# Layer 0 of a two-layer decoder trunk: the latents projected ahead of the last gated tiles and left unscaled, POOL's convolution taps moved to VectorE and 16 of them to TensorE

## The chip, the core and the metric

The kernel runs on one core of a Trainium2 chip. The time is the device time of one launch in microseconds. A core has five engines with a queue each, worked off in order: TensorE (PE, matrix products from SBUF into PSUM), VectorE (DVE), ScalarE (ACT), GpSimd (POOL, which does not touch PSUM here) and SyncE (SP, which issues the transfers). [...]

## What is computed

One sequence of 512 tokens with 1024 channels goes through two layers and a last RMSNorm. The change touches the mixer of layer 0 alone:

```python
def conv_mla_mixer(h, cos, sin, w_in, conv_w, conv_b, conv_ln_g, conv_ln_b,
                   q_norm_g, w_uq, kv_norm_g, w_ukv, w_out):
    proj = h @ w_in                                     # h = rmsnorm(x)
    a, g = proj[..., :512], proj[..., 512:1024]
    u = a * jax.nn.sigmoid(g)
    u = causal_dwconv(u, conv_w, conv_b)                # 31 taps, one filter per channel
    u = jax.nn.silu(layernorm(u, conv_ln_g, conv_ln_b)) # over the 512 channels
    cq, ckv, kr = ...                                   # 384, 256 and 32 columns of proj
    q = (rmsnorm(cq, q_norm_g) @ w_uq)                  # 8 heads of 64 + 32
    kv = (rmsnorm(ckv, kv_norm_g) @ w_ukv)              # 8 heads: 64 keys, 64 values
    ...                                                 # rotary on the 32 parts
    o = mla_attention(qn, qr, kn, kr, v)                # causal, blocks of 128 queries
    return jnp.concatenate([u, o], axis=-1) @ w_out
```

Behind the mixer follow a gated MLP with 2816 channels, a pooling mixer and a second MLP.

## The kernel before

Activations lie channel-major: a tile holds 128 channels by 512 tokens. A product that must be exact is made of three (`mm3`, lines 107 to 109): each operand is split into a rounded part `hi` (ScalarE, L96) and a rest `lo` (VectorE, L97). Weights stream through three buffers, one chunk ahead of the products (`weights`), and every chunk is split on its way. A few products take plain float32 operands in one instruction of the program, which the trace shows as two: scores (L503), values (L548), diagonals (L241) and the key fold (L559).

RMSNorm is applied late: the raw products lie in PSUM, and the factor of each token comes from sums of squares (`Squares`, `rstd`, `rsqrt`) on TensorE and then a chain of eleven tiny VectorE instructions (L192 to L199). `spread` turns a column of factors into rows: four diagonals on VectorE (L240), four products (L241), a copy (L245). `rows0` holds the factor of h.

The order in layer 0 is the order of the code, with the scheduler of the framework placing instructions on each engine by its own estimates:

1. `acc4`: the first two a tiles and the first two g tiles together; meanwhile `r0`, `rows0` and the rotary tables (`rotary`).
2. Four more projections, a and g of the tiles 2 and 3, each pair followed by `glu`.
3. Five projections of latents (`latent`: three of cq, two of ckv). Each is multiplied by `rows0` into a temporary t (L447), split (L101, L102), squared (L211) and summed (L213). The tenth projection is the rotary key.
4. `rstd` of both latents gives `r_q` and `r_kv`; then queries 0 and 1, the keys of the first pair (which need `r_kv` spread over rows), and four value tiles.
5. Eight heads: `scores` with a softmax (reduction with mask L506, its scaled negative L510, exponential L514, normalisation L522), `transposes` of the head before, `values` of the one before that, and the next queries and keys.
6. The output projection (`half`), with the LayerNorm of the convolution between (L614 to L639).

The convolution runs behind all this. `conv(m)` puts the taps of a tile into two lists, which `pump(nd, np_)` hands out at fixed places (`GLU`, `LAT`, `BLK`, `END` taps at a time). A VectorE tap (L367) adds to an accumulator in the PSUM bank `conv`, which ScalarE opens with the last tap and the bias (L361). A POOL tap is a product (L385) and a sum (L387) in SBUF. `close` (L390) adds the two. POOL has 12, 12, 12 and 16 taps of the four tiles, VectorE the other 68.

Of the kernel before, what the change touches and what calls it, by code (L numbers as in the profile page):

```python
# [38 lines left out]
WARM = 40  # L39
POOL_TAPS = (12, 12, 12, 16)  # L40
GLU, LAT, BLK, END = 2, 3, 1, 0


@with_exitstack
def kernel(
# [47 lines left out]

# [1 line left out]
    def split(dst, src):  # L95
# [21 lines left out]
    def rows_of(t, a, b):  # L117
        return t[a:b, 0, :], t[a:b, 1, :]

# [1 line left out]
    stream = (  # L121
        [(w_in0[k], 512) for k in range(KD)]
        + [(w_in1[m], 1024) for m in range(10)]
        + [(w_uq[0], 768), (w_ukv[0], 1024), (w_ukv[1], 1024)]
# [36 lines left out]

# [1 line left out]
    idle = p_c.tile([P, P], mybir.dt.bfloat16, name="idle")  # L163
# [7 lines left out]

# [1 line left out]
    col = p_c.tile([P, N_COL], F32, name="col")  # L173
# [8 lines left out]

# [1 line left out]
    held = []  # L184

    def behind(i):
        """Background work traced from here on starts after instruction i."""
        held[:] = [i]
# [14 lines left out]
    class Squares:  # L203
        """Sums of squares over the channels: tiles are added up, the last one apart."""

# [10 lines left out]

    def rstd(stats, blocks=range(4)):
        ps = aux()
        nb = len(blocks)
        v = small(nb * len(stats))  # L220
        for k, st in enumerate(stats):
            for i, b in enumerate(blocks):
                at = 2 * (nb * k + i)
                for n, t in enumerate(st.parts):
                    pe.matmul(  # L225
                        ps[:, at : at + 2], t[:, b * P : (b + 1) * P], ones[:, 0:2],
                        start=n == 0, stop=n == len(st.parts) - 1,
                    )
            dve.tensor_scalar(
                v[:, nb * k : nb * (k + 1)], ps[:, 2 * nb * k : 2 * nb * (k + 1) : 2],  # L230
                1.0 / st.n, EPS, op0=ALU.mult, op1=ALU.add,
            )
        return rsqrt(v, nb * len(stats))

    def spread_bank(r, blocks=2, tag="aux"):
        """Per-token column to rows: every partition gets the token's value."""
        ps = aux(tag)
        for i in range(blocks):
            d = p_t.tile([P, P], F32, tag="diag", bufs=4, name=uid("d"))
            dve.tensor_scalar(d, ident, r[:, i : i + 1], None, op0=ALU.mult)  # L240
            pe.matmul(ps[:, i * P : (i + 1) * P], ones, d, start=True, stop=True)  # L241
        return ps[:, : blocks * P]
# [6 lines left out]

    # ==== layer 0: conv + latent attention ====  # L250
    p_m = tc.alloc_tile_pool(name="mixer", bufs=1, side="left", reuse_waits="tile")
# [20 lines left out]

    # rotary tables: the turn of each angle from exact products with the digits of 1/(2 pi)
    pos_i = p_t.tile([P, 64], I32, tag="rope_i", bufs=1, name="pos_i")
# [53 lines left out]
    with tc.issue_after(opened.ins):  # L328
        for k in range(KD):
            stat.add(x[k])  # L330
    acc4 = [bank() for _ in range(4)]
    for k in range(KD):
        w = weights(2)
        for m in range(4):
            mm3(acc4[m], part(w, m), pair(xg[k]), k == 0, k == KD - 1)
        if k == 5:
            r0 = rstd([stat])
    rows0 = rows_tile()
# [9 lines left out]

    # depthwise conv, in the background: taps on DVE into PSUM, the rest on ACT and Pool
    u, ys = [], []  # L350
    dve_work, pool_work = [], []

    def conv(m):
# [11 lines left out]

        def dve_tap(j):
            i = dve.scalar_tensor_tensor(  # L367
                st["acc"], u[m][:, j : j + S], c(cw + j), st["acc"],
                op0=ALU.mult, op1=ALU.add,
            )  # L370
            if held:
                tc.add_manual_dep(
                    i.ins, held.pop().ins.name,
                    mybir.DependencyInfo(
                        mybir.DependencyClass.NoSync, mybir.DependencyReason.DATA
                    ),
                    reason="background",
                )

        def pool_tap(j):  # L380
            tap, w = u[m][:, j : j + S], c(cw + j).to_broadcast([P, S])
            t = side
            if j:
                t = p_m.tile([P, S], F32, tag="tapped", bufs=2, name=uid("tapped"))
            pool.tensor_tensor(t, tap, w, op=ALU.mult)  # L385
            if j:
                pool.tensor_tensor(side, side, t, op=ALU.add)  # L387

        def close():
            dve.tensor_tensor(side, st["acc"], side, op=ALU.add)  # L390

        pool_work.extend((lambda j=j: pool_tap(j)) for j in range(POOL_TAPS[m]))
        first = [True]

        def tap(j):
            if first[0]:
                open_acc()
                first[0] = False
            dve_tap(j)
            if j == CW - 2:  # L400
                close()

        dve_work.extend((lambda j=j: tap(j)) for j in range(POOL_TAPS[m], CW - 1))

    def pump(nd, np_):
        for _ in range(min(np_, len(pool_work))):
            pool_work.pop(0)()
        for _ in range(min(nd, len(dve_work))):
            dve_work.pop(0)()

    # GLU branch: u = a * sigmoid(g), kept behind CW - 1 zeros
    def glu(ps_a, ps_g):
# [17 lines left out]
    glu(acc4[2], acc4[3])  # L430
    ps_a = project()
    pump(GLU, 2)
    ps_g = project()
    glu(ps_a, ps_g)
    pump(GLU, 2)
    ps_a = project()
    pump(GLU, 2)
    ps_g = project()
    glu(ps_a, ps_g)
    pump(GLU, 2)  # L440

    def latent(n, gain, width):
        parts, stat = [], Squares(width, dve)
        for m in range(n):
            ps = project()
            t = temp()
            dve.tensor_tensor(t, ps, rows0, op=ALU.mult)  # L447
            parts.append(s4())
            split_scaled(pair(parts[m]), t, c(gain + m))
            stat.add(t)  # L450
            pump(LAT, 2)
        return parts, stat

    cq, stat_q = latent(3, C_QG, 384)
    ckv, stat_kv = latent(2, C_KG, 256)
    # shared rotary key, replicated over the four row groups
    ps = project()
    dve.tensor_tensor(ktab, ktab, rows0, op=ALU.mult)
    kt = temp()
    dve.tensor_tensor(kt, ps, ktab, op=ALU.mult)  # L460
    r = rstd([stat_q, stat_kv])
    r_q, r_kv = r[:, 0:4], r[:, 4:8]
    q_scale = p_s.tile([P, 4], F32, tag="q_scale", bufs=1, name="q_scale")
    dve.tensor_scalar(q_scale, r_q, SCALE, None, op0=ALU.mult)
    pump(2, 2)
    p_xg.release()
# [28 lines left out]
    def scores(h):  # L495
# [4 lines left out]
        for i in range(4):  # L500
# [8 lines left out]
            )  # L509
            dve.scalar_tensor_tensor(  # L510
                nb[:, i : i + 1], mx[:, i : i + 1], -1.0, q_scale[:, i : i + 1],
                op0=ALU.mult, op1=ALU.mult,
            )
            act.activation(  # L514
                p, p, AF.Exp, bias=nb[:, i : i + 1],
                scale=q_scale[:, i : i + 1], accum_out=ls[:, i : i + 1],
            )
            blocks.append(p)
            pump(BLK, 1)
        dve.reciprocal(ls, ls)  # L520
# [53 lines left out]
    for h in range(HEADS):  # L574
# [7 lines left out]
        if h >= 2:  # L582
            values(h - 2)
        pump(END, 1)
    pump(200, 200)

    # output projection: attention half first
    accs = []
# [18 lines left out]
    half(1, att, (0, 1, 2), True, w1)  # L607
    # layernorm over channels, token-major
    mv = p_s.tile([P, 4, 2], F32, tag="mv", bufs=1, name="mv")
# [41 lines left out]
    def residual(ps, m, gain, scale=None, apart=False):  # L651
        """x[m] += ps (scaled); its parts for the next product, and its squares."""
        if scale is None:
# [89 lines left out]
    def last_down(gs, ws):  # L743
        """The last channel tile by halves of the tokens, so that the final norm of the
        first half runs beside the products of the second."""
        m, H = KD - 1, S // 2
# [19 lines left out]
        def last_rstd():  # L766
            """The second half's columns, by a square root that one step refines."""
            v, y, w = small(2), small(2), small(2)
# [43 lines left out]

    # ==== layer 1: windowed means, as band matrices over tokens ====
    first_band = [p_g.tile([P, 4, 256], F32R, tag="g", name=f"first{i}") for i in range(2)]
# [61 lines left out]
def layout(inputs):  # L876
# [8 lines left out]
    def by_col(w):  # L885
        """[K, M] -> [M/128, 128, K/128, 128]: one stationary operand per column tile."""
        K, M = w.shape
# [52 lines left out]

    # constants of the shapes
    turns = np.zeros((P, 6), f32)
# [50 lines left out]
```

## Time and profile before

| | |
|---|---|
| time, three runs | 1034.42 us (1031.65 to 1035.17) |
| span of the profiled execution, first to last instruction | 1028.9 us |
| time of that execution itself | not shown apart from its span |
| busy: TensorE / VectorE / ScalarE / POOL | 989.6 / 607.6 / 399.3 / 189.3 us |
| first score block of head 0 starts (TensorE) | 129.70 us |
| output projection starts | 196.71 us |
| its products with the normalised convolution start | 220.22 us |

The times are of whole launches; the positions in the program are microseconds from the first instruction of the one execution that was profiled. Busy time of TensorE runs over the pipeline, so a full TensorE is one that never waits, and the distance between the starts of two products is the cost of one.

### The profile page before, as it was taken

How to read it: one execution, taken by the hardware profiler on the slowest of the kernel's cores; microseconds unless marked ns; L12 is line 12 of the kernel's file. 1: busy time of each engine (PE TensorE's matmuls, PEld its weight loads, DVE VectorE, ACT ScalarE, POOL GpSimd, SP SyncE). 2: the span in 40 equal slices, each digit the busy share in tenths (PEclk: the TensorE clock that was granted, in tenths of full speed). 3: DMA queues.
4: the chain of work that ended last, by engine and by line, in shares of the span. 5: the costliest groups of instructions: out<-in, count | busy, mean ns of one | idle time of the engine just before them, and what ended most of it. 6: DMA issues, size and time to landing. Idle time of an engine off the chain costs nothing.

```text
span 1028.9 us, 11548 instructions
## 1 busy us (share of the span) xinstructions
PE 989.6 (96%) x4444; PEld 795.5 (77%) x4444; DVE 607.6 (59%) x901; ACT 399.3 (39%) x575; POOL 189.3 (18%) x191
## 2 busy tenths in 40 slices
PE   8996698999999999999999999999999999999996
PEld 6885465677888888888888889888888888888886
DVE  6989899958485556565432337585555655522223
ACT  5423277845253333333222235343333333322221
POOL 4399997004000000000001011300000000000101
PEclk9999699999999999999999999999999999999998
DMA  6422101013222222322222242222323222222212
GB/s 194 169 74 72 36 21 62 21 62 103 97 88 89 95 103 82 103 85 100 100 85 103 84 139 75 82 86 100 102 82 103 83 101 86 99 103 82 103 41 82
DMA packets 29479, 91.99 MB, mean 89 GB/s; under 512 B 4081, under 2 KB 6385, under 8 KB 29425
## 3 DMA queue, kind: packets, MB, share of 16 engines
q1 hardware_dynamic: 28880, 90.74, 25.8%
q8 instruction: 34, 0.56, 0.2%
q10 hardware_dynamic: 544, 0.52, 0.1%
q14 instruction: 21, 0.16, 0.1%
HBM read 89.02 MB, written 2.23 MB: 89 GB/s over the span
## 4 chain that ended last, share of the span: by engine, by line
PE 85%; DVE 11%; issue 1%; DMA 1%; ACT 1%; SPq 0%; DVEq 0%
PE ps L109 27%; PE ps L107 27%; PE ps L108 27%; DVE lo L97 2%; DVE conv L367 1%; DVE s L510 1%; DVE prob L506 1%; PE aux L225 1%; DVE xg L102 1%; PE ps L548 1%; PE aux L241 1%; DMA x<-in_xT_dram 0%; DMA col<-in_cols_dram 0%; DVE s L199 0%; DVE s L197 0%
## 5 line engine op out<-in xcount | busy, mean ns | idle before, releaser
L109 PE MATMUL ps<-xg,lo 128*128 128x512 f32 x816 | 323.8, 397 | 4.0 <-DVE lo L97 4.0
L107 PE MATMUL ps<-xg,hi 128*128 128x512 f32 x816 | 325.1, 398 | 2.0 <-ACT hi L96 2.0
L108 PE MATMUL ps<-xg,hi 128*128 128x512 f32 x816 | 324.2, 397 | 0.0
L96 ACT CAST hi<-raw 128x1024 fp32r<-128x1024 f32 (+2 forms) x166 | 169.6, 1024 | 393.3 <-PE ps L108 350.3
L97 DVE TENSOR_TENSOR lo<-raw,hi 128x1024 fp32r<-128x1024 f32 (+2 forms) x166 | 207.2, 1250 | 163.4 <-ACT hi L96 162.8
L109 PEld LDWEIGHTS ps<-xg,lo 128*128 128x128 f32 x816 | 154.0, 189 | 42.9 <-DVE lo L97 5.7
L107 PEld LDWEIGHTS ps<-xg,hi 128*128 128x128 f32 x816 | 154.3, 189 | 39.6 <-ACT hi L96 2.4
L108 PEld LDWEIGHTS ps<-xg,hi 128*128 128x128 f32 x816 | 154.3, 189 | 37.1
L107 PE MATMUL ps<-g,hi 128*128 128x512 f32 (+1 forms) x374 | 143.1, 383 | 0.0
L108 PE MATMUL ps<-g,hi 128*128 128x512 f32 (+1 forms) x374 | 142.9, 382 | 0.0
L109 PE MATMUL ps<-g,lo 128*128 128x512 f32 (+1 forms) x374 | 142.8, 382 | 0.0
L213 POOL TENSOR_TENSOR sqr<-sqr,sqr 128x512 f32<-128x512 f32 x33 | 51.3, 1553 | 322.7 <-ACT sqr L211 321.4
L688 POOL MEMSET t<- 128x2 f32 x44 | 4.3, 99 | 473.0 <-DVE t L702 362.4
L108 PEld LDWEIGHTS ps<-g,hi 128*128 128x128 f32 x374 | 70.4, 188 | 15.0
L107 PEld LDWEIGHTS ps<-g,hi 128*128 128x128 f32 x374 | 70.3, 188 | 15.0
L109 PEld LDWEIGHTS ps<-g,lo 128*128 128x128 f32 x374 | 70.3, 188 | 15.0
L689 DVE TENSOR_TENSOR t<-ps,rows 128x512 f32<-128x512 f32 x44 | 30.4, 690 | 83.8 <-PE ps L109 83.8
L701 DVE TENSOR_TENSOR t<-ps,rows 128x512 f32<-128x512 f32 x44 | 30.4, 690 | 75.0 <-PE ps L109 75.0
L387 POOL TENSOR_TENSOR side<-side,tapped 128x512 f32<-128x512 f32 x48 | 67.8, 1414 | 1.5
L696 DVE SCALAR_TENSOR_TENSOR t<-t,col,t 128x512 f32<-128x512 f32 x88 | 65.6, 748 | 1.4
L385 POOL TENSOR_TENSOR tapped<-u,col 128x512 f32<-128x512 f32 x48 | 59.8, 1267 | 0.0
L699 ACT ACTIVATE t<-t 128x512 f32<-128x512 f32 x44 | 27.8, 631 | 74.4 <-DVE t L696 74.4
(177 smaller groups left out, 935.4 us busy)
## 6 DMA issues: line engine op xcount, KB each, us to landing
raw<-in_w_up_dram SPq DMA_DIRECT2D x88, 512.0 KB, 3.2
raw<-in_w_down_dram SPq DMA_DIRECT2D x44, 512.0 KB, 3.3
raw<-in_w_in_dram SPq DMA_DIRECT2D x10, 512.0 KB, 3.3
raw<-in_w_out_dram SPq DMA_DIRECT2D x8, 512.0 KB, 3.3
x<-in_xT_dram SPq DMA_DIRECT2D x8, 256.0 KB, 4.3
raw<-in_w_in_dram SPq DMA_DIRECT2D x8, 256.0 KB, 3.6
raw<-in_w_uq_dram SPq DMA_DIRECT2D x4, 384.0 KB, 2.9
out_dram<-g SPq DMA_DIRECT2D x6, 256.0 KB, 2.3
```

The costliest lines, as they stand in the source:

```text
L96: i = act.copy(dst[0], src)
L97: dve.tensor_tensor(dst[1], src, dst[0].bitcast(F32), op=ALU.subtract)
L107: pe.matmul(ps, a[0], b[0], start=start, stop=False)
L108: pe.matmul(ps, a[0], b[1], start=False, stop=False)
L109: pe.matmul(ps, a[1], b[0], start=False, stop=stop)
L213: self.engine.tensor_tensor(self.parts[0], self.parts[0], t, op=ALU.add)
L385: pool.tensor_tensor(t, tap, w, op=ALU.mult)
L387: pool.tensor_tensor(side, side, t, op=ALU.add)
L689: dve.tensor_tensor(ut[:, 2 : 2 + S], pu, rows, op=ALU.mult)
L696: dve.scalar_tensor_tensor(a, ut[:, j : j + S], c(fw + j * NF + f), a, op0=ALU.mult, op1=ALU.add)
L699: act.activation(a, a, AF.Silu)
L701: dve.tensor_tensor(b, pv, rows, op=ALU.mult)
```

## The change

- The latents and the rotary key are projected right after the first four tiles; a and g of the tiles 2 and 3 come behind them. The stream of weights follows.
- Latents are no longer multiplied by `rows0`. Split and square read the raw product in PSUM. Since both r_q and r_kv then belong to unscaled rows, EPS is replaced in their `rstd` by `floor`, EPS times the mean square of x plus EPS, kept from `r0`.
- POOL's taps are gone. VectorE does all taps of the tiles 0 to 2 (the last of each in `open_acc`, as before) and 15 of the tile 3. The first 16 of tile 3 are products on TensorE: POOL builds a diagonal of the tap's weights (128 by 128, four buffers), TensorE multiplies it with the shifted tile into the bank `aux`. `close` is a copy on ScalarE.
- `pump` hands out 3 taps per gated projection, 4 per latent, 2 per score block, and a TensorE tap behind every second score block.
- The scaled negatives of the maxima (L510) are made for two blocks at a time, and the exponentials follow in pairs.

The core of the diff:

```diff
-POOL_TAPS = (12, 12, 12, 16)
-GLU, LAT, BLK, END = 2, 3, 1, 0
+PE_TAPS = 16
+GLU, LAT, BLK, END = 3, 4, 2, 0
...
-        + [(w_in1[m], 1024) for m in range(10)]
+        + [(w_in1[m], 1024) for m in (4, 5, 6, 7, 8, 9, 0, 1, 2, 3)]
...
+            if floor is None:
+                dve.tensor_scalar(vk, cols_of, 1.0 / st.n, EPS, op0=ALU.mult, op1=ALU.add)
+            else:
+                dve.scalar_tensor_tensor(
+                    vk, cols_of, 1.0 / st.n, floor, op0=ALU.mult, op1=ALU.add
+                )
+        if keep is not None:
+            dve.tensor_scalar(keep, v, EPS, None, op0=ALU.mult)
...
+        def pe_tap(j):
+            if j == 0:
+                st["acc"] = aux()
+            d = p_m.tile([P, P], F32, tag="tapped", bufs=4, name=uid("tap"))
+            pool.tensor_scalar(d, ident, c(cw + j), None, op0=ALU.mult)
+            pe.matmul(st["acc"], d, u[m][:, j : j + S], start=j == 0, stop=j == PE_TAPS - 1)
+
+        def tap(j):
+            while m == 3 and pe_work:
+                pe_work.pop(0)()
+            if not st:
+                open_acc()
...
-        def pool_tap(j):
-            tap, w = u[m][:, j : j + S], c(cw + j).to_broadcast([P, S])
-            t = side
-            if j:
-                t = p_m.tile([P, S], F32, tag="tapped", bufs=2, name=uid("tapped"))
-            pool.tensor_tensor(t, tap, w, op=ALU.mult)
-            if j:
-                pool.tensor_tensor(side, side, t, op=ALU.add)
-
         def close():
-            dve.tensor_tensor(side, st["acc"], side, op=ALU.add)
+            bias = c(C_CB + m) if m == 3 else 0.0
+            act.activation(side, st["acc"], AF.Identity, bias=bias, scale=1.0)
+
+        n_pe = PE_TAPS if m == 3 else 0
+        pe_work.extend((lambda j=j: pe_tap(j)) for j in range(n_pe))
+        work.extend((lambda j=j: tap(j)) for j in range(n_pe, CW if m == 3 else CW - 1))
+        work.append(close)
...
-            t = temp()
-            dve.tensor_tensor(t, ps, rows0, op=ALU.mult)
             parts.append(s4())
-            split_scaled(pair(parts[m]), t, c(gain + m))
-            stat.add(t)
-            pump(LAT, 2)
+            split_scaled(pair(parts[m]), ps, c(gain + m))
+            stat.add(ps)
+            pump(LAT)
...
-    r = rstd([stat_q, stat_kv])
+    r = rstd([stat_q, stat_kv], floor=floor)
...
+    for _ in range(2):
+        ps_a = project()
+        pump(GLU)
+        ps_g = project()
+        glu(ps_a, ps_g)
+        pump(GLU)
...
-            pump(BLK, 1)
+            if i % 2:
+                two = slice(i - 1, i + 1)
+                dve.scalar_tensor_tensor(
+                    nb[:, two], mx[:, two], -1.0, q_scale[:, two], op0=ALU.mult, op1=ALU.mult
+                )
+                for n in (i - 1, i):
+                    act.activation(
+                        blocks[n], blocks[n], AF.Exp, bias=nb[:, n : n + 1],
+                        scale=q_scale[:, n : n + 1], accum_out=ls[:, n : n + 1],
+                    )
+            pump(BLK, i % 2)
```

How this moves the queues shows at three places. On VectorE, the chain of the latents before: `s_905` holds the two sums, `d_997` is the first diagonal of r_kv, `ps_953` and `ps_965` are the products of queries 0 and 1, `lo` is a weight split.

```order
L460 TENSOR_TENSOR t_902<-ps_876,ktab 128x512
L229 TENSOR_SCALAR s_905<-aux_904 128x4
L97 TENSOR_TENSOR lo_986<-raw_983,hi_985 128x1024
L229 TENSOR_SCALAR s_905<-aux_904 128x4
L492 TENSOR_TENSOR q_963<-ps_953,ctab_210 128x512
L192 TENSOR_SCALAR s_916<-s_905 128x8
```

And the end of that chain with what now follows it: `q_scale` and the diagonals `d_939` to `d_948`, taps of tile 0 (`conv_494`), and the multiplication of the third g tile with `rows0` (`t_790`).

```order
L199 SCALAR_TENSOR_TENSOR s_710<-s_711,s_710 128x8
L387 SCALAR_TENSOR_TENSOR conv_494<-u_451,col,conv_494 128x512
L455 TENSOR_SCALAR q_scale<-s_710 128x4
L247 TENSOR_SCALAR d_939<-sq,s_710 128x128
L387 SCALAR_TENSOR_TENSOR conv_494<-u_451,col,conv_494 128x512
L97 TENSOR_TENSOR lo_805<-raw_802,hi_804 128x1024
...
L247 TENSOR_SCALAR d_948<-sq,s_710 128x128
L387 SCALAR_TENSOR_TENSOR conv_494<-u_451,col,conv_494 128x512
L418 TENSOR_TENSOR t_790<-ps_765,rows_391 128x512
```

Before, the chain stood behind queries and ahead of the keys; now it stands ahead of the third gated tile, and the taps of tile 0 are between.

On TensorE, the first head before: four score blocks, then the keys of the next pair (`ps_1099`).

```order
L503 MATMUL ps_1058<-keys_944,q_963 128x128
L503 MATMUL ps_1067<-keys_944,q_963 128x256
L503 MATMUL ps_1076<-keys_944,q_963 128x384
L503 MATMUL ps_1085<-keys_944,q_963 128x512
L107 MATMUL ps_1099<-s_805,hi_949 128x512
```

And the first head now, where `aux_1011` is the accumulator of tile 3, `u_873` that tile and `tap_` a diagonal.

```order
L499 MATMUL ps_1005<-keys_886,q_905 128x256
L380 MATMUL aux_1011<-u_873,tap_1012 128x512
L499 MATMUL ps_1017<-keys_886,q_905 128x384
L499 MATMUL ps_1022<-keys_886,q_905 128x512
L380 MATMUL aux_1011<-u_873,tap_1028 128x512
L107 MATMUL ps_1038<-s_613,hi_891 128x512
```

A tap product stands behind the second and the fourth block of a head.

On POOL, the opening now: between the sums of squares of x (`sqr`) stand the first four diagonals, and the rest of its queue in layer 0 are the other twelve.

```order
L213 TENSOR_TENSOR sqr_213<-sqr_213,sqr_227 128x512
L379 TENSOR_SCALAR tap_1012<-sq,col 128x128
L379 TENSOR_SCALAR tap_1028<-sq,col 128x128
L379 TENSOR_SCALAR tap_1080<-sq,col 128x128
L379 TENSOR_SCALAR tap_1096<-sq,col 128x128
L213 TENSOR_TENSOR sqr_213<-sqr_213,sqr_230 128x512
L213 TENSOR_TENSOR sqr_213<-sqr_213,sqr_233 128x512
L379 TENSOR_SCALAR tap_1150<-sq,col 128x128
```

Before, the seven sums of squares stood there together, and 100 products and sums of taps followed.

More of the change, by code (lines that the diff above doesn't have):

```diff
@@ L215, in add, with rstd @@
                 self.parts.append(t)
-    def rstd(stats, blocks=range(4)):
+    def rstd(stats, blocks=range(4), floor=None, keep=None):
         ps = aux()
@@ L228, in rstd @@
                     )
[L229 to L232, printed above, removed]
+            cols_of = ps[:, 2 * nb * k : 2 * nb * (k + 1) : 2]
+            vk = v[:, nb * k : nb * (k + 1)]
+            if floor is None:
[6 more added lines that the diff above has]
+            dve.tensor_scalar(keep, v, EPS, None, op0=ALU.mult)
         return rsqrt(v, nb * len(stats))
@@ L330 @@
             stat.add(x[k])
+    floor = p_s.tile([P, 4], F32, tag="floor", bufs=1, name="floor")
     acc4 = [bank() for _ in range(4)]
@@ L336 @@
         if k == 5:
-            r0 = rstd([stat])
+            r0 = rstd([stat], keep=floor)
     rows0 = rows_tile()
@@ L347, in project @@
         return ps
-    u, ys = [], []
-    dve_work, pool_work = [], []
+    u, ys, work, pe_work = [], [], [], []
     def conv(m):
@@ L364, in open_acc @@
             )
-        def dve_tap(j):
+        def pe_tap(j):
[9 more added lines that the diff above has]
+                open_acc()
             i = dve.scalar_tensor_tensor(
@@ L378, in dve_tap, with pump @@
                 )
-        def pool_tap(j):
-            tap, w = u[m][:, j : j + S], c(cw + j).to_broadcast([P, S])
-            t = side
-            if j:
-                t = p_m.tile([P, S], F32, tag="tapped", bufs=2, name=uid("tapped"))
-            pool.tensor_tensor(t, tap, w, op=ALU.mult)
-            if j:
-                pool.tensor_tensor(side, side, t, op=ALU.add)
-        def close():
[L390 to L409, printed above, removed]
+        def close():
+            bias = c(C_CB + m) if m == 3 else 0.0
[4 more added lines that the diff above has]
+        work.append(close)
+    def pump(nd, np_=0):
+        for _ in range(min(np_, len(pe_work))):
+            pe_work.pop(0)()
+        for _ in range(min(nd, len(work))):
+            work.pop(0)()
     def glu(ps_a, ps_g):
@@ L430 @@
     glu(acc4[2], acc4[3])
[L431 to L440, printed above, removed]
     def latent(n, gain, width):
@@ L464 @@
     dve.tensor_scalar(q_scale, r_q, SCALE, None, op0=ALU.mult)
-    pump(2, 2)
+    for _ in range(2):
[4 more added lines that the diff above has]
+        pump(GLU)
     p_xg.release()
@@ L509, in scores @@
             )
[L510 to L517, printed above, removed]
-            blocks.append(p)
-            pump(BLK, 1)
+            blocks.append(p)
+            if i % 2:
[9 more added lines that the diff above has]
+            pump(BLK, i % 2)
         dve.reciprocal(ls, ls)
@@ L583 @@
             values(h - 2)
-        pump(END, 1)
+        pump(END)
     pump(200, 200)
```

## The prediction

> **What bounds the kernel now.** I read the page first, then busy time by stage, then who waits for whom, then the order of time on VectorE and TensorE in the one stage that matters.
>
> ```profile
> span 1028.9 us, 11548 instructions
> ...
> PE   8996698999999999999999999999999999999996
> DVE  6989899958485556565432337585555655522223
> ...
> POOL 4399997004000000000001011300000000000101
> PEclk9999699999999999999999999999999999999998
> ```
>
> By stretches of 25 us (the columns are PE, weight load, DVE, ACT and POOL busy time with counts, then the granted clock, the DMA share and GB/s):
>
> ```profile
> 75.00:100.00 25.00, 20.06 (x88) 15.28 (x86) 21.81 (x20) 8.60 (x13) 24.77 (x18) 0.96 0.18 58
> 100.00:125.00 25.00, 11.93 (x41) 9.50 (x42) 22.55 (x28) 4.24 (x7) 24.69 (x21) 0.64 0.16 53
> 175.00:200.00 25.00, 23.19 (x106) 15.88 (x105) 24.04 (x65) 22.96 (x55) 0.00 (x0) 1.00 0.12 43
> ```
>
> From 200 us on TensorE is full until the last slice, and nothing in the change reaches there except by arriving earlier. All of the kernel's loose time that the change can touch lies before: between 75 and 125 us TensorE worked 32 of 50 us, its clock fell to 0.64, and VectorE and POOL were both full. The waits of TensorE up to 260 us say for whom:
>
> ```profile
> PE aux L241 <- DVE d L240: 9.5, 1, 9.5
> PE aux L225 <- DVE s L229: 6.5, 1, 6.5
> PE ps L109 <- DVE lo L97: 4.5, 4, 1.6
> PE ps L536 <- ACT prob L522: 2.8, 5, 1.1
> ```
>
> Each row gives the total, how often, and the longest. In order of time (start, duration, engine, line, operation, what stood before it) VectorE shows why:
>
> ```profile
> 78.09 0.69 DVE L390 TENSOR_TENSOR side<-conv,side 128x512 f32<-128x512 f32 x1 [5.43 <-POOL side L387]
> 113.91 1.19 DVE L199 SCALAR_TENSOR_TENSOR s<-s,s 128x8 f32<-128x8 f32 x1
> 133.52 1.25 DVE L510 SCALAR_TENSOR_TENSOR s<-s,q_scale 128x1 f32<-128x1 f32 x1
> 141.14 0.74 DVE L367 SCALAR_TENSOR_TENSOR conv<-u,col,conv 128x512 f32<-128x512 f32 x1
> 178.10 0.74 DVE L367 SCALAR_TENSOR_TENSOR conv<-u,col,conv 128x512 f32<-128x512 f32 x1
> 178.76 0.14 DVE L510 SCALAR_TENSOR_TENSOR s<-s,q_scale 128x1 f32<-128x1 f32 x1
> 213.44 0.16 DVE L199 SCALAR_TENSOR_TENSOR s<-s,s 128x4 f32<-128x4 f32 x1
> ```
>
> Both long waits are for the latents: 6.5 for their sums of squares, which VectorE reaches late, and 9.5 for the small chain that turns these into r_q and r_kv and its diagonals. The steps of the chain are tiny, and still took about 1 us each (1.19 at 113.91) while POOL was busy, against 0.16 at 213.44 when POOL was idle. The one-column L510 took 1.25 beside POOL, 0.14 without it. A convolution tap (L367), which reads only one tensor from SBUF, took 0.74 both times. So POOL's taps cost VectorE more than they save it, and once (78.09) VectorE even stood 5.4 us for POOL itself.
>
> **The change, term by term.** Everything is set against the same profiled execution. The marks and prices come from the order of time on TensorE, on VectorE and POOL, and from the groups by shape (busy time, mean ns):
>
> ```profile
> 28.27 0.95 PE L225 MATMUL aux<-sq,sqr 128*128 128x2 f32 x8
> ...
> 36.91 0.48 PE L108 MATMUL ps<-xg,hi 128*128 128x512 f32 x1
> ...
> 94.06 0.95 PE L225 MATMUL aux<-sq,sqr 128*128 128x2 f32 x8
> ...
> 126.50 0.39 PE L108 MATMUL ps<-lo,s 128*128 128x512 f32 x1
> 126.72 0.39 PE L109 MATMUL ps<-hi,s 128*128 128x512 f32 x1
> ...
> 129.70 2.32 PE L503 MATMUL ps<-keys,q 128*128 128x128 f32 x8
> ...
> 184.19 1.25 PE L536 MATMUL ps<-sq,prob 128*128 128x128 f32 x10
> 185.28 2.32 PE L548 MATMUL ps<-pt,v 128*128 128x512 f32 x8
> 187.44 2.32 PE L503 MATMUL ps<-keys,q 128*128 128x128 f32 x8
> ...
> 196.71 0.48 PE L107 MATMUL ps<-s,hi 128*128 128x512 f32 x1
> ...
> 220.22 0.48 PE L107 MATMUL ps<-s,hi 128*128 128x512 f32 x1
> ```
>
> ```profile
> 16.99 5.01 POOL L213 TENSOR_TENSOR sqr<-sqr,sqr 128x512 f32<-128x512 f32 x3
> ...
> 175.20 1.22 DVE L97 TENSOR_TENSOR lo<-raw,hi 128x1024 fp32r<-128x1024 f32 x1
> ...
> 183.67 0.28 DVE L506 CUSTOM_DVE_ANT_0 prob<-ps,causal 128x128 f32<-128x128 f32 x1
> 189.55 0.26 DVE L506 CUSTOM_DVE_ANT_0 prob<-ps,causal 128x128 f32<-128x128 f32 x1
> 199.78 4.70 DVE L367 SCALAR_TENSOR_TENSOR conv<-u,col,conv 128x512 f32<-128x512 f32 x6
> 204.57 0.69 DVE L390 TENSOR_TENSOR side<-conv,side 128x512 f32<-128x512 f32 x1
> ```
>
> ```profile
> L367 DVE SCALAR_TENSOR_TENSOR conv<-u,col,conv 128x512 f32<-128x512 f32 x68 | 50.9, 749 | 1.0
> L385 POOL TENSOR_TENSOR side<-u,col 128x512 f32<-128x512 f32 x4 | 4.2, 1040 | 20.1 <-DVE u L422 20.1
> L97 DVE TENSOR_TENSOR lo<-raw,hi 128x1024 fp32r<-128x1024 f32 x15 | 22.8, 1521 | 0.3 <-ACT hi L96 0.2
> ...
> L538 ACT COPY pt<-ps 128x512 f32<-128x512 f32 x16 | 8.8, 574 | 1.0 <-PE ps L536 1.0
> ```
>
> *Projections and latents, 36.9 to 129.7 us (first scores).* The latents come first, so r_kv and its diagonals are asked for four products before the keys need them: the two long waits have 20 us of product behind which to hide. What then fills TensorE: ten projections of 24 products, which ran from 36.91 to 94.06 with one wait of about 1.5 in them (lo L97), so 56; two sums of under 1; 18 query products, 6 for keys, 24 for values at 0.23 (126.50 to 126.72), 11; the key fold and the spread of r_kv, 2. That is 71 us against 92.8, and the scores start at about 108: **-21.9**. The cover for this is VectorE. Its order of work up to the third gate (23 to 27 taps, eight weight splits, the glu and latent steps) adds up to 41 to 45 us from about 36, so about 80; the product it then needs ends at about 82. The cover is there, but thin: another 5 us on VectorE would reach TensorE. The removed scaling (five L447) and the four closes on VectorE are worth about 6 us there at 0.6 to 0.7 each (204.57), and without POOL the 1024-column split falls from its mean of 1.52 to 1.22 (175.20).
>
> *Attention, 129.7 to 196.7 us, 67 us before.* Two things are added. TensorE gets 16 plain float32 products of 512 columns. The values take 2.16 us for 1280 columns (185.28 to 187.44), so 0.86 each, 13.8 in all, two in each head. VectorE gets taps: 105 in the whole against 68 before, of which 51 fall into the heads. A tap after something else goes on after 0.66 (178.10 to 178.76), a tap after a tap after 0.78 (six in 4.70); I take 0.70. The rest of a head on VectorE I take from the head between 183.67 and 189.55, where POOL is idle: 5.88, less three taps, one close and one split, 2.4. With keys, queries and splits, VectorE's eight heads come to 72 us. TensorE's: scores 2.16, two taps 1.7, transposes 1.1 (184.19 to 185.28), values 2.16, query 2.1, keys 1.4 where they occur: 71. By heads (in the order of the changed kernel) TensorE has 7.4, 7.1, 10.7, 9.2, 10.7, 9.2, 7.1, 9.3 and VectorE 7.3, 7.3, 10.1, 10.0, 11.0, 9.0, 8.4, 12.3. The longer in each head sums to 76: **+9**. ScalarE, with 22.96 of 25 busy at 175 to 200 us, gets the close of each tile (0.6, as L538) and nothing else of size; a bubble of 2.7 in the fourth head, where the third tile's opening stands behind four exponentials, is in VectorE's 10.0.
>
> *The tail, 196.7 to 220.2 us.* After the heads VectorE still owes 11 taps in a row, 8.6, and ScalarE a close, 0.8. Before, VectorE closed at 205.3 and the products of the normalised tiles began at 220.22, 15 us later; the changed order moves 12 products (2.8) ahead of the second transposes, so 12.2. From 108: 76 + 8.6 + 0.8 + 12.2 gives 205.5 against 220.2: **-14.7 in sum**. TensorE's own path to the layernorm transposes ends within 1 us of VectorE's, so neither has slack there.
>
> *Small terms.* POOL builds 16 diagonals of 128 columns. The nearest row is the 512-column product, 1.04; the lower end is a quarter of that. The first four stand ahead of the last two sums of squares of x: at most 4.2 late, while that sum, done at 22.0 (16.99 + 5.01), is first used at 28.3, so nothing on TensorE, though a weight split beside them may lose up to 1: I take 0. Unscaled latents need r corrected by the floor (one tiny op, 0.2, hidden) and are read by ScalarE and VectorE straight from PSUM, freeing banks late; the banks come round after six tiles, 34 us: 0. The DMA queue issues the same transfers in the order of use, none moved past another of size.
>
> The 12 later builds run beside the heads. Before, L510 beside POOL was longer by up to 1.1; only operations with two SBUF inputs suffered, and of these the changed heads have 16 L509 and five weight splits among some 130. I take 0.5, between 0 and 12.5 (every build blocks VectorE for 1.04). [...]
>
> Three queues in order do not meet each head's maximum without loss. Before, TensorE stood five times for the normalised probabilities (L536), 2.8 us, in heads that two other engines shared as evenly. I add 2: **-13**. The span would be 1016. The time of the run profiled is not shown beside its span; 5.5 us lie between the 1028.9 and the median of 1034.4, which I keep: 1021.4.
>
> **Rivals.**
> 1. *VectorE gives it back.* It carries 37 more taps and is the longer engine in five heads and in the tail. If each tap costs 0.78 and each head loses another 1 us waiting, attention is 76 + 4 + 8 = 88 and the tail 1 longer: -2, or -5 with half of it, so 1031. For it: VectorE is 22 to 24 of 25 busy in every window above. Against: half the taps alternate with other work.
> [...]
> 3. *Slower.* The diagonal products stand between the score blocks in TensorE's order; with four buffers for the diagonals, each product from the fifth waits for a build that starts only when an older one is used. Two are needed per head of 9 us, so a build must take over 4.7 us to be the bound, and over 5.8 (12 times 1.1 more) to eat the 13; 7 us would give 1049. Against: 1.04 for four times the columns.
> 4. *All hidden.* Every engine overlaps as it could and the TensorE work alone counts (-18): 1016.
> 5. *The waits go elsewhere.* r_kv is early, but TensorE stands for late weight splits (4.5 us of waits today, up to 260 us) because VectorE is behind by 20 us: no change.
>
> **Chances.** The forecast (1016 to 1026) 0.58, the first rival 0.17, the fourth 0.09, the second 0.05, the fifth 0.04, the third 0.07. Less than 0.3%, 3.1 us, can't be told from no change here. Faster is the forecast, the fourth and most of the first: 0.82; same is 0.10, slower 0.08. The range for 8 in 10 reaches from the fourth rival's side to the first's: 1014 to 1030.
>
> **What would show it.** Right: scores start at 106 to 111 us; no TensorE wait above 2 us between 40 and 125, the clock at 1.0 there; the chain's steps at 0.2; POOL nearly empty; heads take 74 to 80 us; layernorm transposes at 191 to 196. Wrong: TensorE waiting for lo L97 or for conv in the projections, builds of several us on POOL, or VectorE still at its last 11 taps while TensorE has been idle for more than 3 us.

## The result and the profile after

The changed kernel takes 1015.76 us (median of four runs, 1015.17 to 1016.66), the kernel before 1033.93 (four runs, 1031.65 to 1035.17): a ratio of 0.9826, with a 95% interval from 0.9812 to 0.9840. Faster by 18.2 us; 13.0 had been forecast (1021.4 us, range 1014 to 1030). The measured time lies inside that range and 0.2 us below the narrower one of 1016 to 1026.

From the page of the changed kernel:

```profile
span 1013.7 us, 11538 instructions
...
PE 995.8 (98%) x4476; PEld 798.7 (79%) x4476; DVE 591.7 (58%) x914; ACT 399.7 (39%) x578; POOL 71.3 (7%) x107
...
PE   8999999999999999999999999999999999999996
...
DVE  6999989856765555555332338485555555522323
...
POOL 6000100022000000000000103100000000000111
PEclk9999999999999999999999999999999999999998
...
PE 93%; DVE 4%; issue 1%; DMA 1%; SPq 0%; ACT 0%; DVEq 0%
```

TensorE carries 93% of the chain that ended last, the row of its clock stays at 9 up to the last slice, and POOL is nearly empty. VectorE is busy 15.9 us less than before (607.6 to 591.7), though it does 37 taps more. The same kernel by stretches (columns as before):

```profile
75.00:100.00 25.00, 25.00 (x107) 19.85 (x106) 22.73 (x38) 9.97 (x13) 0.00 (x0) 1.00 0.23 69
100.00:125.00 25.00, 25.00 (x104) 17.50 (x104) 23.65 (x56) 17.47 (x41) 3.70 (x5) 1.00 0.13 43
```

Where TensorE had worked 32 of 50 us, it works 50. Its four largest waits up to 260 us:

```profile
PE ps L107 <- ACT hi L96: 2.1, 2, 1.9
PE aux L248 <- DVE d L247: 1.7, 1, 1.7
PE ps L109 <- DVE lo L97: 1.4, 2, 0.8
PE aux L637 <- DVE t L626: 1.3, 1, 1.3
```

None is for the latents (the L248 here is the opening's rows0, at 35.58). The marks, from the order of time on TensorE and VectorE:

```profile
106.54 0.82 PE L499 MATMUL ps<-keys,q 128*128 128x128 f32 x4
107.20 1.02 PE L380 MATMUL aux<-u,tap 128*128 128x512 f32 x2
108.06 0.81 PE L499 MATMUL ps<-keys,q 128*128 128x384 f32 x2
...
176.96 0.48 PE L107 MATMUL ps<-s,hi 128*128 128x512 f32 x1
...
204.07 1.21 PE L107 MATMUL ps<-s,hi 128*128 128x512 f32 x4
```

```profile
75.55 0.17 DVE L199 SCALAR_TENSOR_TENSOR s<-s,s 128x8 f32<-128x8 f32 x1
...
180.25 8.65 DVE L387 SCALAR_TENSOR_TENSOR aux<-u,col,aux 128x512 f32<-128x512 f32 x11
...
217.68 2.09 DVE L652 TENSOR_TENSOR x<-ps,x 128x512 f32<-128x512 f32 x3 [9.96 <-PE ps L109]
```

The scores start at 106.54 (129.70 before), the heads end and the output projection starts at 176.96 (196.71), the products with the normalised convolution start at 204.07 (220.22). So 23.2 us are gained before the heads, 3.4 of it is paid back in them (70.4 us against 67.0) and 3.6 in the tail (27.1 against 23.5). That leaves 16.1; the span is shorter by 15.2, and the 0.9 between was not followed further. A chain step takes 0.17 where it took 1.19. A TensorE tap, which the trace shows as two instructions, takes 0.86 (107.20 to 108.06).

### The profile page after: what moved, and what is told of

Same layout as the page of the kernel before. It is cut to its first block, busy times and chain, and to the rows that moved or that the text cites. A ratio compares the mean times of both kernels' runs of the same rounds, so it can differ in the third digit from the quotient of the medians.

```text
span 1013.7 us, 11538 instructions
## 1 busy us (share of the span) xinstructions
PE 995.8 (98%) x4476; PEld 798.7 (79%) x4476; DVE 591.7 (58%) x914; ACT 399.7 (39%) x578; POOL 71.3 (7%) x107
## 4 chain that ended last, share of the span: by engine, by line
PE 93%; DVE 4%; issue 1%; DMA 1%; SPq 0%; ACT 0%; DVEq 0%
PE ps L107 28%; PE ps L109 28%; PE ps L108 28%; PE ps L499 2%; PE ps L546 2%; DVE lo L97 1%; PE aux L380 1%; PE ps L534 1%; PE aux L248 1%; PE aux L226 1%; DVE xg L102 1%; DMA x<-in_xT_dram 0%; DMA col<-in_cols_dram 0%; PE ps L860 0%; PE ps L861 0%
## 5 line engine op out<-in xcount | busy, mean ns | idle before, releaser
L96 ACT CAST hi<-raw 128x1024 fp32r<-128x1024 f32 (+2 forms) x166 | 169.6, 1024 | 400.6 <-PE ps L108 373.0
L97 DVE TENSOR_TENSOR lo<-raw,hi 128x1024 fp32r<-128x1024 f32 (+2 forms) x166 | 201.7, 1217 | 165.0 <-ACT hi L96 165.0
L108 PEld LDWEIGHTS ps<-g,hi 128*128 128x128 f32 x374 | 70.4, 188 | 15.0
L109 PEld LDWEIGHTS ps<-g,lo 128*128 128x128 f32 x374 | 70.4, 188 | 15.0
L107 PEld LDWEIGHTS ps<-g,hi 128*128 128x128 f32 x374 | 70.4, 188 | 15.0
L387 DVE SCALAR_TENSOR_TENSOR conv<-u,col,conv 128x512 f32<-128x512 f32 x90 | 67.5, 750 | 1.6 <-ACT conv L370 0.5
L102 DVE SCALAR_TENSOR_TENSOR xg<-x,col,xg 128x512 fp32r<-128x512 f32 x32 | 32.7, 1038 | 12.1 <-ACT xg L101 12.1
L107 PE MATMUL ps<-s,hi 128*128 128x512 f32 x96 | 39.1, 421 | 0.0
```

What stands on the lines that cost most here:

```text
L96: i = act.copy(dst[0], src)
L97: dve.tensor_tensor(dst[1], src, dst[0].bitcast(F32), op=ALU.subtract)
L102: dve.scalar_tensor_tensor(dst[1], src, scale, dst[0].bitcast(F32), op0=ALU.mult, op1=ALU.subtract)
L107: pe.matmul(ps, a[0], b[0], start=start, stop=False)
L108: pe.matmul(ps, a[0], b[1], start=False, stop=False)
L109: pe.matmul(ps, a[1], b[0], start=False, stop=stop)
```

## The experiments

Each ratio is to the runs of the kernel before that were made in the same series, whose medians lie between 1033.8 and 1034.6 us; differences to the kernel before are taken within a series. The last two columns are positions in the profiled execution: the first scores, and the first product with the normalised convolution.

| kernel | us, median (range) | ratio to before, 95% | scores | products |
|---|---|---|---|---|
| before | 1033.93 (1031.65 to 1035.17) | | 129.70 | 220.22 |
| after | 1015.76 (1015.17 to 1016.66) | 0.9826 [0.9812, 0.9840] | 106.54 | 204.07 |
| order_only | 1021.50 (1020.92 to 1022.25) | 0.9884 [0.9866, 0.9903] | 113.44 | 209.80 |
| taps_only | 1019.39 (1018.84 to 1019.98) | 0.9862 [0.9841, 0.9884] | 106.97 | 207.53 |
| pool_two | 1031.61 (1030.18 to 1033.96) | 0.9981 [0.9967, 0.9995] | 120.91 | 219.34 |
| pool_one | 1016.15 (1015.51 to 1018.23) | 0.9832 [0.9809, 0.9854] | 106.99 | 204.52 |
| pe8 | 1023.49 (1022.00 to 1024.29) | 0.9902 [0.9882, 0.9921] | 106.64 | 210.54 |
| pe20 | 1015.70 (1015.21 to 1016.10) | 0.9824 [0.9805, 0.9842] | 106.65 | 204.29 |
| pe24 | 1019.17 (1018.83 to 1020.06) | 0.9863 [0.9845, 0.9881] | 106.46 | 207.55 |
| lat5_pe12 | 1018.94 (1017.32 to 1019.32) | 0.9852 [0.9830, 0.9874] | 107.75 | 206.40 |
| late_unscaled | 1020.66 (1019.13 to 1021.20) | 0.9869 [0.9843, 0.9895] | 107.05 | 207.52 |
| late_filled | 1013.76 (1013.37 to 1014.85) | 0.9807 [0.9788, 0.9825] | 106.91 | 202.49 |
| late_pe13 | 1015.34 (1014.15 to 1015.73) | 0.9820 [0.9803, 0.9836] | 106.44 | 203.47 |
| unpaired | 1015.04 (1014.41 to 1016.12) | 0.9820 [0.9797, 0.9842] | 105.97 | 203.24 |

### order_only: the latents ahead, POOL's taps kept

```diff
 # before.py, with the rstd(floor, keep) of after.py; the loop over the last
 # four gated tiles stands behind r_q and r_kv, as in after.py
-        + [(w_in1[m], 1024) for m in range(10)]
+        + [(w_in1[m], 1024) for m in (4, 5, 6, 7, 8, 9, 0, 1, 2, 3)]
...
-            t = temp()
-            dve.tensor_tensor(t, ps, rows0, op=ALU.mult)
-            split_scaled(pair(parts[m]), t, c(gain + m))
+            split_scaled(pair(parts[m]), ps, c(gain + m))
```

> The kernel before with the latents moved ahead and left unscaled; POOL keeps its 52 taps, all pumps as before. Measured so far: before 1033.9, after 1015.8 us, the first scores at 129.7 and 106.5 us. Theory A (the two long waits of TensorE, 9.5 and 6.5 us, are a matter of order, and hide behind the four gated projections though VectorE is still stretched by POOL): the chain's steps stay at about 1.1 us each, the scores start at 113 to 118 us, 1019 to 1024 us. Theory B (the sharing of VectorE's time with POOL is what costs: with POOL's taps in place VectorE stays behind, and TensorE stands for weight splits instead): scores at 122 us or later, TensorE waits of 5 us or more for lo L97, 1029 to 1034 us. Theory C (order alone is the whole gain): 1017 us or less.

It gained 12.3 us, with the scores at 113.4: theory A. Its waits of TensorE between 36 and 113.4 us, where the scores start, and two of VectorE's groups between 36 and 125 us:

```profile
PE ps L107 <- DVE t L422: 1.6, 1, 1.6
PE ps L108 <- DVE lo L97: 1.4, 1, 1.4
PE ps L109 <- DVE lo L97: 0.8, 1, 0.8
PE aux L248 <- DVE d L247: 0.2, 1, 0.2
```

```profile
L198 DVE SCALAR_TENSOR_TENSOR s<-s,s 128x8 f32<-128x8 f32 x3 | 3.4, 1132 | 0.1
L102 DVE SCALAR_TENSOR_TENSOR s<-ps,col,s 128x512 fp32r<-128x512 f32 x5 | 3.7, 744 | 0.2 <-ACT s L101 0.2
```

The two waits for the latents, 6.5 and 9.5, are gone although a chain step still took up to 1.1 us: the order does hide them (the 0.2 is the opening's rows0, at 36.13). Theory B's waits for weight splits did not grow: 2.2 us here, 2.1 before in the same stage. The last line shows a side effect: read from PSUM instead of from t, the latent's split takes 0.74 us beside POOL; in the kernel before, with both inputs in SBUF, it took 1.62.

### taps_only: the latents late and scaled, POOL's taps gone

The order_only edit undone in after.py; taps, pumps and pairs stay as changed.

> The changed kernel with the latents back behind all gated tiles and scaled by rows0 as before; taps on VectorE and 16 on TensorE, maxima in pairs. Theory A (each part removes its own share): the chain's steps fall to 0.17 us, so the wait of 9.5 us for its diagonals shrinks to 2 or less, that for the sums of squares (6.5 us) stays above 2; TensorE pays 13.8 us for its taps; scores at 114 to 120 us, 1023 to 1029 us. Theory B (contention is what costs): no wait over 2 us is left though the order is the old one, 1016 to 1020 us. Theory C (order is all): 1030 us or more.

The scores start at 107.0, within 0.4 us of the changed kernel, with the latents in their old place. That is theory B's 1016 to 1020, not the 1023 to 1029 of theory A. With POOL quiet, VectorE reaches the latents' sums and steps in time even where only the queries stand between. The two cures are worth 12.3 and 14.4 alone and 18.2 together: they remove the same waits, and either one alone gives two thirds of the gain or more.

### pool_two and pool_one: POOL made busy again, doing nothing useful

The order on the four other engines is that of the changed kernel, instruction by instruction.

```diff
+    def busy():
+        for _ in range(5):                       # pool_one: 4
+            b = p_m.tile([P, S], F32, tag="busy", bufs=2, name=uid("busy"))
+            pool.tensor_tensor(b, u[0][:, :S], causal, op=ALU.mult)
+            # pool_one: pool.tensor_scalar(b, u[0][:, :S], c(C_CB), None, op0=ALU.mult)
             pump(LAT)
+            busy()                               # and behind each pump(GLU)
```

> The changed kernel plus 45 idle POOL products of 128x512 with two SBUF inputs during the projections, whose result nobody reads; the other engines' instructions and their order are those of the changed kernel. Theory A (sharing stretches VectorE's operations with two SBUF inputs, and VectorE has 7 us to spare between 36 and 106): splits of 1024 columns 1.5 us instead of 1.22, the chain's steps 0.7 to 1.1 instead of 0.17, in all 10 to 16 us on VectorE, of which 3 to 9 come through: 1019 to 1027 us. Theory B (the stretched steps hide, since the waits are for the order of the work and the latents come early): 1015 to 1017.5 us. Theory C (as much as before lost): over 1028 us.

> The same with 36 idle POOL instructions of one SBUF input (tensor_scalar, 128x512, the form that builds the diagonals) instead. Theory A (any POOL instruction that reads SBUF stretches VectorE): like pool_two, 1019 us or more, chain steps over 0.5 us. Theory B (it takes two inputs on POOL as well): chain steps at 0.17, splits 1.22, 1015 to 1017 us.

The two-input products cost 15.8 us of the 18.2 (1031.6, theory C, above A's bounds); the one-input ones cost nothing that shows (theory B). The groups by shape between 36 and 125 us, of pool_two:

```profile
L412 POOL TENSOR_TENSOR busy<-u,causal 128x512 f32<-128x512 f32 x45 | 66.0, 1506 | 15.9 <-DVE u L431 15.9
L387 DVE SCALAR_TENSOR_TENSOR conv<-u,col,conv 128x512 f32<-128x512 f32 x43 | 32.2, 749 | 0.6
L97 DVE TENSOR_TENSOR lo<-raw,hi 128x1024 fp32r<-128x1024 f32 x10 | 16.2, 1616 | 0.5 <-ACT hi L96 0.5
L247 DVE TENSOR_SCALAR d<-sq,s 128x128 f32<-128x128 f32 x5 | 3.7, 732 | 0.0
L199 DVE SCALAR_TENSOR_TENSOR s<-s,s 128x8 f32<-128x8 f32 x3 | 3.6, 1215 | 0.1
L423 DVE TENSOR_TENSOR t<-ps,rows 128x512 f32<-128x512 f32 x4 | 2.7, 684 | 0.2 <-ACT rows L252 0.2
```

and of pool_one:

```profile
L412 POOL TENSOR_SCALAR busy<-u,col 128x512 f32<-128x512 f32 x36 | 64.9, 1822 | 15.9 <-DVE u L431 15.9
L97 DVE TENSOR_TENSOR lo<-raw,hi 128x1024 fp32r<-128x1024 f32 x10 | 12.5, 1248 | 1.6 <-ACT hi L96 1.5
L247 DVE TENSOR_SCALAR d<-sq,s 128x128 f32<-128x128 f32 x7 | 1.8, 279 | 0.0
L199 DVE SCALAR_TENSOR_TENSOR s<-s,s 128x8 f32<-128x8 f32 x3 | 0.8, 269 | 0.1
```

POOL was busy for 65 us in both. Beside two-input products a split takes 1.62 and a step 1.22; beside one-input ones 1.25 and 0.27 (alone 1.22 and 0.17). What reads a PSUM operand is the same in all (a tap 0.75 us, L423 and in the changed kernel L418 0.68 to 0.69). The operations of pool_one read SBUF too (u) and hardly stretch VectorE. The latents stand ahead in pool_two, and still TensorE loses 14.4 us before the heads. 9.7 of it are waits, for weight splits and others, and behind two of them its granted clock fell for a while (means of 0.60 from 76 to 80 us, where its products then start 0.43 us apart instead of 0.23, and of 0.79 and 0.78 from 112 to 120). The largest waits between 36 and 120.9 us:

```profile
PE ps L109 <- DVE lo L97: 4.5, 3, 2.4
PE ps L107 <- DVE t L423: 2.4, 1, 2.4
PE aux L226 <- DVE s L235: 2.2, 1, 2.2
```

In order_only the same order kept most of its gain beside a busy POOL. VectorE did less there: 34 taps before the scores against 39, and 73.3 us of work before them against 82.5 in pool_two. This fits an order that hides the chain only as long as VectorE has time left; no run varied that alone.

### pe8, pe24, pe20: which engine sets the end

One constant: PE_TAPS = 8, 24, 20 instead of 16.

> The changed kernel with 8 taps on TensorE instead of 16, so VectorE does 8 more. Theory A (TensorE and VectorE are balanced within about 1 us at the layernorm transposes, 190.9 us, and either one moved later sets the end): VectorE's 8 taps at 0.70 each make the last run of taps end 5.6 us later, at 194.5, and the transposes begin at 195 to 196: 4 to 5 us slower, 1019.5 to 1021 us, with a new wait of TensorE for the close. Theory B (TensorE's work alone sets the end, VectorE has room): 8 x 0.86 = 6.9 us faster, 1009 us. Theory C (VectorE has half of that in its own small gaps): within 1.5 us of 1015.8.

> The changed kernel with 24 taps on TensorE instead of 16, so VectorE does 8 fewer. Theory A (balanced, either one sets the end): TensorE's 8 more products at 0.86 come on top, 6.9 us slower, 1022 to 1023 us, with VectorE's last run of taps 3 long instead of 11 and standing idle before the transposes. Theory B (VectorE sets the end, at 0.70 to 0.78 a tap): 5 us faster, 1010 us. Theory C (a mixture): within 1.5 us of 1015.8.

> The changed kernel with 20 taps on TensorE. pe24 was 3.4 us slower and pe8 7.7 us. Theory A (two straight limits: TensorE's 0.86 a tap to the one side, and to the other VectorE, with the 2.1 us that TensorE still waits in the layernorm at 16 taps as the first to be filled): 4 x 0.86 = 3.4, less the 2.1 of wait and the 1 us or so that the tail absorbed in pe24: 1016 to 1017.5 us, no wait in the layernorm. Theory B (VectorE is the longer one at 16, so four taps fewer on it pay): 1013 to 1015 us.

pe8 is 7.7 us slower, pe24 3.4, pe20 as fast: both engines are at the bound, with a flat bottom from 16 to 20 taps. Eight more products moved the last scores by 6.8 us (170.77 to 177.56), but the products of the normalised tiles by 3.5: the tail had that much slack on TensorE, 2.1 of it in the layernorm's waits.

pe8 was to cost 4 to 5. One part of the rest is VectorE: its last tap ended at 197.0 instead of 188.9, so 8.1 us later and not 5.6. The other shows by stretches of 4 us:

```profile
192.00:196.00 4.00, 2.25 (x10) 1.49 (x8) 3.66 (x5) 1.04 (x1) 0.00 (x0) 1.00 0.80 243
196.00:200.00 4.00, 1.21 (x5) 0.81 (x5) 2.19 (x4) 1.13 (x2) 0.00 (x0) 0.75 0.45 140
200.00:204.00 4.00, 1.97 (x8) 1.57 (x8) 2.67 (x12) 1.90 (x4) 0.00 (x0) 0.50 0.00 0
...
208.00:212.00 4.00, 3.34 (x14) 2.79 (x13) 1.29 (x2) 3.91 (x7) 0.10 (x1) 0.50 0.00 0
```

TensorE stood for the close (3.5 us) and for the layernorm (4.1), and its granted clock fell to 0.50 (200 to 212 us). From the first product with the normalised convolution to the first sum with x it took 13.6 us in the changed kernel (204.07 to 217.68) and 15.6 in pe8 (210.54 to 226.15): 2 us more for the same products. So here such waits were paid for once more, in part, in the products behind them. Not every wait was followed by that: the 1.3 and 0.8 in the layernorm of the changed kernel left the clock at 1.00 (196 to 208 us), but behind a wait of 3.1 in late_unscaled, below, it was at 0.50, and in pool_two, behind a single wait of 2.2 (L226, up to 74.70), at a mean of 0.60 from 76 to 80 us.

### lat5_pe12: more taps in the projections

```diff
-PE_TAPS = 16
-GLU, LAT, BLK, END = 3, 4, 2, 0
+PE_TAPS = 12
+GLU, LAT, BLK, END = 3, 5, 2, 0
```

> The changed kernel with 12 taps on TensorE instead of 16 and five taps per latent instead of four. Theory A (VectorE has 7 us of gaps between 36 and 106 us, so that five taps more fit there; TensorE saves 4 x 0.86 = 3.4 us in the heads, VectorE has 4 - 5 = -1 tap after 106): scores still at 106.5 to 107.5, 1013 to 1015 us. Theory B (VectorE is full there, and the taps push the rest back): VectorE's last run of taps ends 2.8 us later, 1018 to 1020 us, as pe8 (8 taps fewer on TensorE) was 7.7 us slower.

3.2 us slower, theory B. Counted in the order of time, 43 taps are done at 107 us, as in the changed kernel: the gaps between VectorE's operations there are not room for five more.

### late_unscaled, late_filled, late_pe13: what the place of the latents is worth

```diff
 # late_unscaled: after.py, the loop over the last four gated tiles ahead of the latents again
 # late_filled: late_unscaled and
     ckv, stat_kv = latent(2, C_KG, 256)
+    pump(4)
     ...
     dve.tensor_tensor(kt, ps, ktab, op=ALU.mult)
+    pump(3)
 # late_pe13: late_filled and
-PE_TAPS = 16
+PE_TAPS = 13
```

> The changed kernel with the latents back behind all gated tiles as before, but left unscaled (the order of taps_only, 1019.4 us, without its five multiplications by rows0). taps_only started its scores at 107.0 us, as early as the changed kernel (106.5), and lost its 3.6 us later, where VectorE's last tap ended 4.1 us later. Theory A (what is left of the latents' part is VectorE's work: five multiplications of 0.69 are 3.4 us, and the place of the latents is worth nothing once POOL is quiet): 1015 to 1017 us, TensorE's wait in the layernorm 1 to 2 us. Theory B (the place is what counts): 1019 to 1020 us.

> late_unscaled (1020.7 us, latents behind the gated tiles) with seven more taps handed out around the last latents and the rotary key. There VectorE did no tap between 89 and 100 us (31 done at 90 and at 100), waiting for TensorE's last latents, and had 38 taps done at 107 us against 43 of the changed kernel; its last tap ended 4.1 us later. Theory A (the place of the latents is worth only these five taps of VectorE): with 42 to 44 taps done at 107 us the last tap ends at 188.5 to 190, TensorE waits 1 to 2 us in the layernorm, 1015.5 to 1017 us. Theory B (the late order costs by something else, such as the chain of r_q and r_kv standing before the first head): the hole closes, and the time stays at 1019 to 1021 us. Theory C (the taps delay the sums of squares and with them r_kv): scores later than 108 us, over 1021 us.

late_unscaled did not gain on taps_only: the five multiplications were hidden, theory A's sum was wrong. Its VectorE shows by what (in brackets the idle time before, and who ended it):

```profile
90.09 0.69 DVE L213 TENSOR_TENSOR sqr<-sqr,sqr 128x512 f32<-128x512 f32 x1 [0.73 <-ACT sqr L211]
92.23 0.69 DVE L458 TENSOR_TENSOR t<-ps,ktab 128x512 f32<-128x512 f32 x1 [1.45 <-PE ps L109]
95.08 0.16 DVE L235 SCALAR_TENSOR_TENSOR s<-aux,floor 128x4 f32<-128x4 f32 x1 [0.75 <-PE aux L226]
96.12 0.69 DVE L489 TENSOR_TENSOR q<-ps,ctab 128x512 f32<-128x512 f32 x1 [0.88 <-PE ps L109]
...
191.41 1.55 DVE L387 SCALAR_TENSOR_TENSOR aux<-u,col,aux 128x512 f32<-128x512 f32 x2
```

No tap is handed out to it there, and it waits for the last latents; the taps left over end at 193.0 instead of 188.9. TensorE waits for it in the layernorm, and its clock (third column from the right) is at half behind that:

```profile
PE aux L638 <- DVE t L627: 3.1, 1, 3.1
```

```profile
204.00:208.00 4.00, 3.34 (x15) 2.68 (x14) 1.45 (x4) 2.93 (x5) 0.10 (x1) 0.50 0.21 86
```

With seven taps in that hole (late_filled) this wait is gone, and the kernel is 6.9 us faster than late_unscaled and 2.0 faster than the changed kernel, at 1013.76 us; the ranges of the two do not touch, their intervals against before overlap. It did better than theory A's 1015.5 to 1017, with 41 taps at 107 us. So what the place of the latents gives once POOL is quiet is work for VectorE in one hole, and that can be had without moving them.

> late_filled (1013.8 us) with 13 taps on TensorE instead of 16. In late_filled TensorE waits nowhere between 60 and 205 us, and VectorE stands 2.9 us for TensorE before the layernorm's statistics. Theory A (there TensorE is now the longer by about 3 us, and three taps moved back fit VectorE's gap): 3 x 0.86 = 2.6 less on TensorE, 3 x 0.70 = 2.1 more on VectorE, 1011 to 1012.5 us. Theory B (balanced already, any shift shows as a wait and then a lower clock): 1014 to 1017 us.

late_pe13 came out 1.6 us above late_filled in the median, theory B; the ranges touch (1014.15 to 1015.73 against 1013.37 to 1014.85), so the size is not sure. In its trace TensorE's waits in the tail came back (0.8 and 0.4), and 1.3 for probabilities; its granted clock stayed at 1.00 from 192 to 212 us, so the lower clock of theory B was not shown. VectorE's 2.9 us there were not free.

### unpaired: the maxima block by block

```diff
-            if i % 2:
-                two = slice(i - 1, i + 1)
+            one = slice(i, i + 1)            # L509 and the exponential in each block
```

> The changed kernel with the scaled negatives of the maxima made block by block (32 of one column instead of 16 of two), each exponential behind its own. Theory A (VectorE is as long as TensorE in the heads, and each further tiny operation takes 0.08 to 0.15 us of it): 16 x 0.08 to 0.15 = 1.3 to 2.4 us more on VectorE, of which the last run of taps carries most to the layernorm: 1016.5 to 1018.5 us. Theory B (earlier exponentials shorten the bubble of 1.7 us in the fourth head and the wait for the last probabilities by as much): 1015 to 1016.3 us.

1015.04 us, theory B: the 16 tiny operations saved are not seen in the time.

## Why the prediction was right, and where it was not

- *Projections and latents, -21.9.* Measured -23.2; the sum of TensorE's work (71 us) was right, and so was its end at about 108 (106.5). The reason given is one of two, and not the one that this kernel needs. I wrote that the latents come first and the two waits get 20 us of product behind which to hide. That works by itself (order_only, scores at 113.4), but taps_only reaches 107.0 without it, and pool_two loses 14.4 us with it. With the changed kernel's taps on VectorE it is the end of POOL's two-input products that carries the gain, and of that the sum had only the weight splits that fall from 1.52 to 1.22, as cover.
- *The thin cover.* Right: five taps more, some 3.5 us, already move the scores by 1.2 (lat5_pe12), and beside a loud POOL the cover is far too thin (pool_two).
- *Attention, +9, and the loss between queues, +2.* These two terms failed. By heads I took the longer of the two engines, 76, and added 2; the heads took 70.4, 3.4 more than before and not 11, and so TensorE's own sum of 71. With 20 and 24 taps on TensorE they took 73.9 and 77.3, its 0.86 more per tap. The sign that heads take 74 to 80 us failed with these terms, and the layernorm transposes came early too (the first at 186.5, the next at 190.9, for 191 to 196); the other signs came out. VectorE's taps are not tied to their head: a late one moves to the tail and delays nobody until the close (13 of them ended there, 11 were forecast). *The tail* was mis-sized the other way: 21.6 forecast, 27.1 measured. Heads and tail together came to 97.5 (106.54 to 204.07), against 97.6 in the sum without the loss. That the two errors cancel so nearly is luck, as the sum did not foresee it. The last 11 taps took 8.65 (8.6 forecast), a TensorE tap 0.86.
- *The term outside the span, 5.5.* Wrong: the runs of the changed kernel lie 1.8 to 1.9 us above their spans. Those of the kernel before, shown later with their spans, lie 1.8 to 2.9 above them, but the spans themselves run from 1028.9 to 1033.6; the execution profiled was as short as the shortest. That is why the time fell by 18.2 and the span by 15.2. With 1.8 the forecast would have been 1017.8, so this term alone put it 3.7 us too high.
- *Builds, opening.* In the heads a build takes 0.60 us, the first one 1.29; the four in the opening take 3.91 together. TensorE waited for none. They delay the sum of x to 25.4, first used at 26.2: hidden, as costed.
- *The rivals.* The third fell with the builds (0.60 us each in the heads). The fifth is what pool_two shows, 5.1 us of waits for late splits before the scores, but only with POOL busy with two-input products. The first is seen in pe8, 8 taps further on: VectorE does give it back from there. Half of its extra 13 us would have given -8, not the -5 written there. The fourth had the right number for the time (1016) by luck: pe8 with less TensorE work is slower, and its -18 was not reached in the span (-15.2), and the 5.5 above, which it carries too, made up for that.

## What to carry to other kernels

Before an order is changed to hide a stretched chain, ask what stretches it: here the engine beside it did, and its silence was worth as much as the hiding. Two cures for one wait did not add up (12.3 and 14.4 us alone, 18.2 together). When two engines are balanced, move work only into a hole that the trace shows on one of them, and count a longer wait of TensorE (here falls of the clock, to 0.50 in pe8, followed some waits of 1.77 us and more) with the products that it may slow afterwards.

## What the runs showed of the hardware

- Beside GpSimd instructions of one SBUF input (pool_one, 1.82 us for 512 columns) VectorE's split of 1024 columns took 1.25 us (1.22 alone) and a step of the chain (L199) 0.27 (0.17 alone); beside those of two (pool_two, 1.51) they took 1.62 and 1.22.
- It was not only VectorE's operations with two SBUF inputs that suffered, as I had written: the diagonals of L247, with one tile and one column as inputs, went from 0.28 to 0.73 in pool_two, and those of L240 in the kernel before took 0.60 in the mean between 36 and 130 us, beside POOL, against a median of 0.28 over the whole execution.
- The length of a wait alone did not decide whether TensorE's clock fell. In the opening TensorE waits once for a rounded weight (hi L96). Waits of 1.77 us (late_pe13), 1.97 (pool_one), 1.98 (before), 2.22 (pe20), 2.35 (late_filled) and 2.47 (lat5_pe12) were followed by a mean clock of 0.57 to 0.75 between 16 and 20 us, and waits of 1.89 (pe24), 1.93 (after), 2.06 (late_unscaled) and 2.49 (taps_only) by 1.00.
- The spans of the kernel before vary by 4.7 us from run to run with a mean granted clock from 0.981 to 0.986, those of the changed kernel, in four runs, by 1.4 at 0.995 to 0.996. What makes this spread was not shown; no run was made for it.
